# Spreading the block sums over the heads, and moving the meta rows' table and their part of the state, in a hybrid convolution and retention trunk

## The chip, the cores and the metric

The kernel runs on 1 core of one Trainium2 chip. The metric is the device time of one execution in microseconds (us); the time before is the median of 3 runs. In the profile PE is TensorE's matmuls, PEld its weight loads, DVE is VectorE, ACT ScalarE, POOL GpSimd and SP SyncE, which here only issues DMAs ("SPq" in a timeline).

## The reference

One decoder layer over 2048 rows of 1024 values, all f32. Sixteen learned "meta" rows are put in front of the sequence; they feed the branches and are not part of the output.

```python
hn = rms_norm(concat(meta, x), norm1_g)
cx, cb, cc, cg, q, k, v, rg = split(hn @ w_in, 8)        # w_in: 1024 x 4096
conv_out = cb * causal_conv3(cc * cx) * silu(cg)         # 512 channels
ret = head_group_norm(retention_chunkwise(rotary(q) * d**-0.5, rotary(k), v))
ret_out = ret * silu(rg)                                 # 4 heads of 128
y = h + concat(conv_out, ret_out) @ w_out
return rms_norm(y, final_g)[:, 16:]
```

Retention runs over chunks of 128 rows: inside a chunk with a decaying causal mask, between chunks through a 128 x 128 state for each head. The meta rows give every head's first state.

## The kernel before

**Products.** Activations lie transposed, 128 channels by 512 rows (HB). Each f32 operand is split into a high part and a low remainder (`split`, L85: an ACT copy that rounds, then a DVE subtraction, L114), and a product is three matmuls: low x high, high x low, high x high (L217 in `quad`, L273 in `quad_plain`). The split of a weight makes the tiles `wh` and `wl`, that of an activation `mh` and `ml`. `quad` computes a 2 x 2 block product with seven products in place of eight, as Strassen and Winograd do. For that it needs sums of blocks on both sides: those of the weights are made by POOL in `stationary` (four operations a quad, in place, in the buffers `ra` and `sa`), those of the activations by `block_sums`. A quad's results are taken out of PSUM by `take`; three of its banks are copied to tiles `tc` by ACT (L224), and PE may go on writing such a bank only after its copy.

**Order of work.** The 2048 rows are done in two halves, r = 0 and 1. In each half eight units follow one another, in the order of `UNITS`: units 0 to 3 are the retention heads (`head`), units 4 to 7 the groups of the convolution (`group_plain` for the first one, `conv_group` for the others). The first half begins with unit 4, and goes on with 0, 1, 2, 3, 5, 6, 7; the second runs from 0 to 7. A unit is two quads, plus, in a head, the small matmuls of retention, which mix with the next unit's first quad. After both halves the output projection follows (`output`, eight pairs of row blocks).

**Sums made ahead.** The activations' sums for the second half, and those of w_out for the output, are made while earlier units run. `prepare` (L183) is a generator with four steps. A step loads four blocks (L372 or L379), runs `block_sums` (with a scale, for x: one ACT multiplication, L178, three DVE operations of L175 and one subtraction; without, for w_out: four subtractions) and stores four results to DRAM (L191, `sums_x` or `sums_w`). The main loop draws steps from it at the end of a unit (L920 to L922): two at each unit from 3 up until the four are used up, and none at the unit with which the first half begins. In the first half these are the units 3 and 5, in the second 3 and 4. At the same place `conv_group` units of the first half draw the row factors of the second half: loads of x (L331) and squares on ACT (L332), four groups after unit 5. `prepared` (L194) loads the finished sums back (L201) and splits them.

**The meta rows in a head.** In the first half `ahead` loads the next unit's weights and multiplies the meta rows with them (`meta_products`, L408 on PE; the result is copied to the tile `mk`). `meta_state` (L423) loads the head's rotary table for the meta rows into a tile `mr` (L426; it shares the four buffers of the tag `tc`), adds up halves of the products (`meta_sums`, two L111), applies the rotary (L431 twice, L432, L111), multiplies keys and values on PE (L435) and copies the result to `state[h]` (L436). It is called behind the head's second quad (L681), but nothing holds its instructions there: the scheduler may put them on their engines' queues as soon as their operands are there.

**V across.** A head needs v with rows and channels exchanged. `part` (L599) splits the f32 values into planes of 16 bits (ACT, L602) and turns them with a transposing DMA (`cross`, L595, issued by SP); `join` puts them together again (L669). In the second half's first unit (`first` is given, L639) a `quad_plain` runs, `part` is called from its `take`, and after it `between` (L644) calls `prepared(m, sums_x, (0, 2))`, eight loads and splits for the second quad.

**Order.** Instructions are given in program order; a scheduler with a timing model sets the order of each engine's queue from priorities (program order), readiness and free buffers, and adds the semaphores. An engine runs its queue in order: what waits holds up all behind it. `tc.issue_after(i)` asks that the instructions of its block which run on i's engine are queued behind i; it waits for nothing itself. Buffers are shared by tag: `g` has 16 (`gen`), `ra` 8, `tc` 4.

The second quad's last gate product is L660, `sg[j] = pp * f[0]`, in the second `take` of `head`.

Of the kernel before, what the change touches and what calls it, by code (L numbers as in the profile page):

```python
# [8 lines left out]
F32 = mybir.dt.float32  # L9
# [4 lines left out]
ALU = mybir.AluOpType  # L14

P = 128
D = 1024
SEQ = 2048
NMETA = 16
KT = D // P  # L20
NG = 4
EPS = 1e-6
HB = 512
# [5 lines left out]
RING, RAW, GEN, COPIES = 3, 8, 16, 4  # L29
# [5 lines left out]
SUMS = (3, 2, 4, 6)  # L35

UNITS = (4, 0, 1, 2, 3, 5, 6, 7), (0, 1, 2, 3, 4, 5, 6, 7)


def retention_constants():  # L40
# [31 lines left out]
def hybrid_trunk(ctx: ExitStack, tc: tile.TileContext, t, out: bass.AP, chunk_decay):  # L72
# [5 lines left out]
    nc = tc.nc  # L78
# [4 lines left out]
    sb = ctx.enter_context(tc.tile_pool(name="sb", bufs=2))  # L83
# [100 lines left out]
    def prepare(load, dst, scale=None):  # L184

        for kt in range(KH):
# [4 lines left out]
                nc.sync.dma_start(dst[n, kt], a)  # L191
            yield

    def prepared(m, src, ns, held={}):  # L194

        for n in ns:
            for kt in range(KH):
                a = held.get((n, kt))
                if a is None:
                    a = gen("t")[:, :HB]  # L200
                    nc.sync.dma_start(a, src[n, kt])  # L201
                parts(m, SUMS[n], kt, a)

    copied = [None]
# [161 lines left out]
    def gain_of(k):  # L366
        return gain[:, k : k + 1]
# [52 lines left out]
        add(nc.vector, c, c, d)  # L420
        return a, c, b, d

    def meta_state(h, scratch):  # L423

        rot = sb.tile([P, HB], F32, name="mr", tag="tc", bufs=COPIES)[:NMETA, : 2 * P].rearrange("p (a c) -> p a c", a=2)
        nc.sync.dma_start(rot, t["rot_m"][h])  # L426
        k, v, a, b = meta_sums(scratch)
        half = P // 2
        lo, hi = slice(0, half), slice(half, P)
        for i, j in ((lo, hi), (hi, lo)):  # L430
            nc.vector.tensor_tensor(out=b[:, i], in0=k[:, j], in1=rot[:, 1, i], op=ALU.mult)  # L431
        nc.vector.tensor_tensor(out=a, in0=k, in1=rot[:, 0], op=ALU.mult)  # L432
        add(nc.vector, k, a, b)
        up = ps_misc()
        nc.tensor.matmul(up[:, :P], k, v, start=True, stop=True)  # L435
        nc.scalar.copy(out=state[h], in_=up[:, :P])  # L436
# [157 lines left out]
    def cross(across, apart):  # L594
        nc.sync.dma_start(  # L595
            across.bitcast(U16).rearrange("p (c f) -> p c f", c=2 * CH), apart.bitcast(U16), transpose=True
        )

    def part(a):  # L599

        apart, across = gen("pl")[:, :HB], gen("tr")[:, :HB]
        nc.scalar.copy(out=planes(apart), in_=halves(a))  # L602
        cross(across, apart)
        return across

    waiting = [[], []]
# [9 lines left out]
    def head(h, r, m, rot_t, f, turning, blocks, ahead, first=(), between=()):  # L616


        between = iter(between)
        k, v, late = [None, None], [None, None], []  # L620
        tables = [rot_t[:, :, j * HB : (j + 1) * HB] for j in range(2)]

        def take(i, j, pp, c):
            if i == 1 and c is None:
                v[j] = part(pp)
                return
            d = gen("kv")[:, :HB]
            if c is None:
                nc.scalar.copy(out=d, in_=pp)
            else:  # L630
                add(nc.vector, d, pp, c)
            if i == 0:
                rotary(d, tables[j])
                k[j] = d
            else:
                v[j] = d
                late.append(j)
# [3 lines left out]
        else:  # L641
            quad(stationary(blocks[0]), m, take)
            catch_up(0)
        next(between, lambda: None)()  # L644
        q, sg = [None, None], [None, None]

        def take(i, j, pp, c):
            d = gen("qg")[:, :HB]
            if i == 0:
                if c is None:  # L650
                    nc.scalar.copy(out=d, in_=pp)
                else:
                    add(nc.vector, d, pp, c)
                rotary(d, tables[j])
                q[j] = d
            else:
                if c is not None:
                    add(nc.vector, d, pp, c)
                    pp = d
                nc.vector.tensor_tensor(out=d, in0=pp, in1=f[0][:, j * HB : (j + 1) * HB], op=ALU.mult)  # L660
                sg[j] = d

        def split_late():
# [14 lines left out]
            join(1)  # L678
        next(between, lambda: None)()
        if blocks[1]:  # L680
            meta_state(h, blocks[1])  # L681
        blocks = ahead()
        states = [state[h]]
        vt = []
        for j in range(2):
# [12 lines left out]
            for c in range(CH - last):  # L698
                nxt = sb.tile([P, P], F32, name="state", tag="state", bufs=2 * CH)
                nc.vector.scalar_tensor_tensor(  # L700
                    out=nxt, in0=states[-1], scalar=chunk_decay[h], in1=up[:, c * P : (c + 1) * P],
# [4 lines left out]
        for j in range(2):  # L706
            sc = ps_misc()
            for c in range(CH):
# [4 lines left out]
                out=pm.rearrange("p (c i) -> p c i", c=CH), in0=sc.rearrange("p (c i) -> p c i", c=CH),  # L713
# [128 lines left out]
    for r in range(NR):  # L842
        f = factors[r]
        rot_t = sb.tile([P, 2, BLK], F32, name="rot_t", tag="rot_t", bufs=1)
        p0 = NMETA + r * BLK

        def load_tables():
            nc.sync.dma_start(rot_t, t["rot"][:, :, p0 : p0 + BLK])

        if r == 0:  # L850
            w = [None] * 4
            loads = w_loads(2 * NG)

            def begin(half):
                for n in (half, 2 + half):
                    w[n] = plain_part(n, loads[n], FIRST_W)

            m, b = moving(
                load_x(r), gain_of, {(0, 0): lambda: begin(0), (0, KH - 1): lambda: begin(1), (0, KT - 1): normalise_meta}
            )  # L860
            first = [[p for a, p in w]]
            blocks = None, meta_products([a for a, p in w])
            first.append(plain_parts(w_loads(2 * NG + 1)))
            load_tables()
            nc.sync.dma_start(cols, t["cols"])
            t3 = [a[:, i * HB : (i + 1) * HB] for a in (row_tile("t3", 1) for _ in range(2)) for i in range(2)]
            t1 = [brief("t1") if n < BRIEF else sb.tile([P, HB], F32, name="t1", tag="tc", bufs=COPIES) for n in range(KH)]
            for kt in range(KH):
                b11, b21, b12, b22 = (b[n * KH + kt] for n in range(4))
                block_sums(b11, b12, b22, b21, t1[kt], t3[kt], gain_of(kt), gain_of(KH + kt), nc.gpsimd)  # L870
                parts(m, 2, kt, b22)
                parts(m, 6, kt, b21)
            for _ in row_factors(0, f):
                pass
            nc.sync.dma_start(causal, t["causal"])
            nc.sync.dma_start(conv_w, t["conv_w"])
            nc.sync.dma_start(ret_g, t["ret_norm_g"])

            def late_parts():
                for i, held in ((3, t1), (4, t3)):  # L880
                    for kt in range(KH):
                        parts(m, i, kt, held[kt])

            between = ()
            later = prepare(load_x(1), sums_x, gain_of)
        else:
            m, b = moving(load_x(r), gain_of)
            first = [plain_parts(w_loads(0))]
            load_tables()
            prepared(m, sums_x, (1, 3))  # L890
            between = (lambda: prepared(m, sums_x, (0, 2)),)
            blocks = None, None
            later = prepare(load_w_out, sums_w)
        steps = row_factors(r + 1, factors[r + 1]) if r < NR - 1 else iter(())
        units = UNITS[r]
        turning = None
        special = (first, between)
        for n, unit in enumerate(units):
            following = units[n + 1] if n + 1 < len(units) else None
            rest = lambda: ahead(r, following, early=n == 0)  # L900
            if r + n == 0:
                blocks, completion = group_plain(unit - NG, m, f, blocks[1], first, late_parts, rest)
                special = (), completion
            elif unit < NG:
                if turning is None:
                    turning = [row_tile(name, 1 - r) for name in ("apart", "across")]
                blocks = head(unit, r, m, rot_t, f, turning, blocks, rest, *(special if unit == 0 else ()))
            else:
                if r == NR - 1 and following is None:
                    idle = sb.tile([P, 2, BLK], F32, name="held", tag="rot_t", bufs=1)  # L910
                    areas = [idle[:, 0], idle[:, 1], row_tile("held", 0), row_tile("held", 0)]
                    for i, a in enumerate(areas):
                        for j in range(2):
                            n, kt = 2 * (i // 2), i % 2 * 2 + j
                            held[n, kt] = a[:, j * HB : (j + 1) * HB]
                            nc.sync.dma_start(held[n, kt], sums_w[n, kt])
                blocks = conv_group(unit - NG, r, m, f, blocks, rest)
                for _ in range(4 - r):
                    next(steps, None)
            if NG - 1 <= unit and r + n > 0:  # L920
                next(later, None)
                next(later, None)  # L922

    m, b = moving(load_w_out)
# [42 lines left out]
```

## Time and profile before

| | |
|---|---|
| median of 3 runs | 887.63 us (886.71 to 888.54) |
| the profiled execution's own time | 887.77 us |
| its span, first to last instruction | 886.0 us |
| mean granted TensorE clock | 0.996 |
| DVE, ACT, POOL busy | 718.5, 472.3, 395.2 us |
| first half's heads, units 0 to 3 | from 57 to 245 us of the span |
| unit 5 of the first half | from 245 to 297 us |
| second half's units 0 to 3, unit 4 | from 378 to 561, from 561 to 608 us |

The page groups instructions by line, engine and operation; names such as `wl<-ra,wh` are tiles of the program, output first. A group's "idle" is time in which its engine did nothing just before its instructions, with what ended it. A timeline gives the start and duration of instructions in order, and in brackets the idle time before one and its releaser. Durations come from one profiled execution. Since PE is busy nearly throughout, idle time of the other engines costs nothing unless PE ends up waiting for it.

### The profile page before, as it was taken

The page shows a single profiled execution, that of the slowest core. Times are in us where ns is not written, and L with a number is a line of the kernel's source. Part 1 is how long each engine was busy: PE and PEld are TensorE (multiplying, and loading weights), DVE is VectorE, ACT ScalarE, POOL GpSimd, SP SyncE. Part 2 cuts the span into 40 slices and gives each one's busy share as a digit, 9 for nine tenths or more (in the row PEclk, how much of TensorE's full clock was granted, in tenths as well). Part 3 has the DMA queues.
Part 4 walks back from the last instruction along what each step waited for, and adds up shares of the span by engine and source line. Part 5 has one row for each costly group of instructions (what it writes and reads, how often), then busy time and mean ns, then how long its engine had stood idle before and what let it go on. Part 6 is the DMA issues. An engine that isn't in the chain of part 4 may idle for free.

```text
span 886.0 us, 12731 instructions
## 1 busy us (share of the span) xinstructions
PE 867.5 (98%) x4279; PEld 712.9 (80%) x4279; DVE 718.5 (81%) x1176; ACT 472.3 (53%) x871; POOL 395.2 (45%) x291
## 2 busy tenths in 40 slices
PE   8999999999999999999999999998999999999996
PEld 6778788878887778887888888887888888788885
DVE  6788888888897966998888898998767699766764
ACT  8665437373646463746464645534334476555553
POOL 0554241323145454451233323254547455877763
PEclk9999999999999999999999999999999999999999
DMA  9713223231577643935142423867221493555532
GB/s 338 235 56 80 72 62 91 66 96 48 141 264 224 205 153 79 293 124 158 48 103 65 91 77 78 268 194 256 60 72 53 136 381 108 177 157 180 165 112 91
DMA packets 110033, 125.31 MB, mean 141 GB/s; under 512 B 41424, under 2 KB 58128, under 8 KB 109968
## 3 DMA queue, kind: packets, MB, share of 16 engines
q1 hardware_dynamic: 109968, 124.50, 45.6%
q8 instruction: 34, 0.56, 0.3%
q14 instruction: 31, 0.25, 0.1%
HBM read 90.92 MB, written 25.17 MB: 131 GB/s over the span
## 4 chain that ended last, share of the span: by engine, by line
PE 74%; DVE 9%; DMA 3%; issue 3%; ACT 2%; POOL 1%; SPq 1%; POOLq 0%; DVEq 0%; ACTq 0%
PE pj L217 64%; PE pj L273 2%; PE ms L720 2%; DVE wl L114 2%; DVE ml L114 2%; PE ms L721 2%; PE ms L710 2%; PE ms L697 1%; DMA w<-in_w_out 1%; DVE x L175 1%; DVE c L470 1%; PE ms L408 1%; PE ms L688 1%; DVE w L114 1%; DMA n<-in_x 1%
## 5 line engine op out<-in xcount | busy, mean ns | idle before, releaser
L217 PE MATMUL pj<-mh,wl 128*128 128x512 f32 x1008 | 398.6, 396 | 6.6 <-ACT tc L224 2.8
L217 PE MATMUL pj<-ml,wh 128*128 128x512 f32 x1008 | 393.7, 391 | 1.1 <-DVE ml L114 1.1
L217 PE MATMUL pj<-mh,wh 128*128 128x512 f32 x1008 | 393.8, 391 | 0.0
L102 ACT CAST wh<-ra 128x512 fp32r<-128x512 f32 x216 | 133.7, 619 | 261.1 <-PE pj L217 217.2
L217 PEld LDWEIGHTS pj<-mh,wl 128*128 128x128 f32 x1008 | 189.7, 188 | 50.1 <-ACT tc L224 4.4
L217 PEld LDWEIGHTS pj<-mh,wh 128*128 128x128 f32 x1008 | 189.6, 188 | 40.1
L217 PEld LDWEIGHTS pj<-ml,wh 128*128 128x128 f32 x1008 | 189.7, 188 | 39.9 <-DVE ml L114 1.6
L114 DVE TENSOR_TENSOR wl<-ra,wh 128x512 fp32r<-128x512 f32 x216 | 185.2, 859 | 36.8 <-ACT wh L102 36.3
L114 POOL TENSOR_TENSOR ra<-ra 128x512 f32<-128x512 f32 x72 | 112.1, 1557 | 93.9 <-PE ms L408 42.4
L114 POOL TENSOR_TENSOR ra<-sa,ra 128x512 f32<-128x512 f32 x36 | 53.2, 1479 | 108.5 <-DVE wl L114 105.0
L111 POOL TENSOR_TENSOR sa<-ra 128x512 f32<-128x512 f32 x36 | 51.8, 1440 | 83.8 <-DMA ra<-in_w_in 32.4
L224 ACT COPY tc<-pj 128x512 f32<-128x512 f32 x108 | 62.6, 579 | 0.0
L273 PE MATMUL pj<-ml,mh 128*128 128x512 f32 x128 | 50.3, 393 | 0.0
L273 PE MATMUL pj<-mh,mh 128*128 128x512 f32 x128 | 50.1, 394 | 0.0
L273 PE MATMUL pj<-mh,ml 128*128 128x512 f32 x128 | 48.8, 398 | 0.1
L733 POOL TENSOR_TENSOR rp<-rs,neg_half 128x4 f32<-128x4 f32 x16 | 17.8, 1113 | 52.9 <-DVE rs L111 52.8
L783 DVE TENSOR_TENSOR yo<-pj,yo 128x512 f32<-128x512 f32 x32 | 21.9, 686 | 18.5 <-POOL yo L111 10.9
L533 POOL TENSOR_TENSOR c<-c,rr 128x512 f32<-128x512 f32 x14 | 27.6, 1973 | 20.7 <-DVE c L470 11.4
L785 ACT ACTIVATE rot<-yo 128x512 f32<-128x512 f32 x32 | 20.2, 630 | 30.7 <-DVE yo L783 30.3
L533 POOL TENSOR_TENSOR c<-c,tc 128x512 f32<-128x512 f32 x14 | 26.9, 1919 | 20.5 <-ACT tc L560 20.5
L102 ACT CAST wh<-sa 128x512 fp32r<-128x512 f32 x36 | 22.1, 615 | 23.4 <-PE pj L217 23.4
L788 POOL TENSOR_TENSOR z<-yo,final_g 128x512 f32<-128x512 f32 x16 | 26.9, 1684 | 16.5 <-DVE yo L783 16.5
(138 smaller groups left out, 1190.9 us busy)
## 6 DMA issues: line engine op xcount, KB each, us to landing
ra<-in_w_in SPq DMA_DIRECT2D x128, 256.0 KB, 2.8
x<-in_xT SPq DMA_DIRECT2D x48, 256.0 KB, 4.8
w<-in_w_out SPq DMA_DIRECT2D x32, 256.0 KB, 5.2
ra<-mixed SPq DMA_DIRECT2D x32, 256.0 KB, 2.9
yo<-in_x SPq DMA_DIRECT2D x32, 256.0 KB, 4.3
ra<-in_x SPq DMA_DIRECT2D x16, 256.0 KB, 3.3
mixed<-c SPq DMA_DIRECT2D x16, 256.0 KB, 2.6
mixed<-qg SPq DMA_DIRECT2D x16, 256.0 KB, 2.3
```

What stands on the lines that cost most here:

```text
L102: nc.scalar.copy(out=hi, in_=src)
L111: eng.tensor_tensor(out=out, in0=a, in1=b, op=ALU.add)
L114: eng.tensor_tensor(out=out, in0=a, in1=b, op=ALU.subtract)
L217: nc.tensor.matmul(bank, a[:, ks], b, start=first and kt == 0 and n == 0, stop=kt == KH - 1 and n == 2, skip_group_check=not first,)
L224: copied[0] = nc.scalar.copy(out=c, in_=bank)
L273: nc.tensor.matmul(banks[i], a[:, ks], b, start=half + kt + n == 0, stop=half == 1 and kt == KH - 1 and n == 2,)
L533: eng.tensor_tensor(out=out, in0=a, in1=b, op=ALU.mult)
L710: nc.tensor.matmul(sc[:, cs], k[j][:, cs], q[j][:, cs], start=True, stop=True)
L733: nc.gpsimd.tensor_tensor(out=rp, in0=rs, in1=neg_half.rearrange("p (c a) -> p c a", a=1), op=ALU.pow)
L783: last[0] = nc.vector.tensor_tensor(out=y, in0=pp, in1=y, op=ALU.add)
L785: nc.scalar.activation(junk, y, AF.Square, accum_out=ss[:, i, j : j + 1])
L788: nc.gpsimd.tensor_tensor(out=ys[i][j], in0=y, in1=final_g[:, j * HB : (j + 1) * HB], op=ALU.mult)
```

## The change

It has four parts. (1) `prepare` is drawn one step at a time, behind the units that `MAKES_SUMS` lists: in the first half units 0, 1, 2 and 5, in the second 0, 1, 2 and 4. (2) `mr` gets a tag and a tile of its own, and its load is issued at the top of `head`, ahead of the first quad. (3) `meta_state`'s instructions on DVE are queued behind the last gate product. (4) In the second half's first unit the two transposes of v are queued on SP behind the last of the eight loads of `prepared`.

```diff
+MAKES_SUMS = (0, 1, 2, 5), (0, 1, 2, 4)
...
+    loaded = [None]
+
     def prepared(m, src, ns, held={}):
...
-                    nc.sync.dma_start(a, src[n, kt])
+                    loaded[0] = nc.sync.dma_start(a, src[n, kt])
...
-    def meta_state(h, scratch):
-
-        rot = sb.tile([P, HB], F32, name="mr", tag="tc", bufs=COPIES)[:NMETA, : 2 * P].rearrange("p (a c) -> p a c", a=2)
+    def meta_table(h):
+        rot = sb.tile([P, 2, P], F32, name="mr", tag="mr", bufs=1)[:NMETA]
         nc.sync.dma_start(rot, t["rot_m"][h])
+        return rot
+
+    def meta_state(h, scratch, rot):
+
...
-    def part(a):
+    def part(a, to_cross=None):
...
-        cross(across, apart)
+        if to_cross is None:
+            cross(across, apart)
+        else:
+            to_cross.append((across, apart))
         return across
...
+        to_cross, gated = [], [None]
         k, v, late = [None, None], [None, None], []
+        rot = meta_table(h) if blocks[1] else None
...
-                v[j] = part(pp)
+                v[j] = part(pp, to_cross if len(first) else None)
...
         next(between, lambda: None)()
+        if to_cross:
+            with tc.issue_after(loaded[0].ins):
+                for pair in to_cross:
+                    cross(*pair)
...
-                nc.vector.tensor_tensor(out=d, in0=pp, in1=f[0][:, j * HB : (j + 1) * HB], op=ALU.mult)
+                gated[0] = nc.vector.tensor_tensor(out=d, in0=pp, in1=f[0][:, j * HB : (j + 1) * HB], op=ALU.mult)
...
         if blocks[1]:
-            meta_state(h, blocks[1])
+            with tc.issue_after(gated[0].ins):
+                meta_state(h, blocks[1], rot)
...
-            if NG - 1 <= unit and r + n > 0:
-                next(later, None)
+            if unit in MAKES_SUMS[r]:
                 next(later, None)
```

## The prediction

> **What bounds the kernel now.** I read the page's totals by engine first, then the waits of PE, then PE's timeline at every pause, then the other engines' timelines at the pauses that the change can touch.
>
> ```profile
> PE 867.5 (98%) x4279; PEld 712.9 (80%) x4279; DVE 718.5 (81%) x1176; ACT 472.3 (53%) x871; POOL 395.2 (45%) x291
> ```
>
> PE works for 867.5 us of a span of 886.0. The change removes no matmul, so all that it can win lies in the other 18.5 us. The waits of PE give 2.3 us at the start:
>
> ```profile
> PE ms L826 <- ACT warm L820: 2.3, 1, 2.3
> ```
>
> The timeline of PE shows the pauses inside. The bracket holds the idle time and what ended it.
>
> ```profile
> 63.31 0.50 PE L217 MATMUL pj<-mh,wl 128*128 128x512 f32 x1 [1.03 <-ACT tc L224]
> 94.46 0.46 PE L435 MATMUL ms<-mk 16*128 16x128 f32 x2 [0.94 <-DVE mk L111]
> 106.92 0.47 PE L217 MATMUL pj<-mh,wl 128*128 128x512 f32 x1 [0.54 <-DVE wl L114]
> 286.77 0.50 PE L217 MATMUL pj<-mh,wl 128*128 128x512 f32 x1 [1.81 <-ACT tc L224]
> 303.38 0.47 PE L217 MATMUL pj<-mh,wl 128*128 128x512 f32 x1 [0.72 <-ACT tc L560]
> 411.94 0.50 PE L217 MATMUL pj<-ml,wh 128*128 128x512 f32 x1 [1.14 <-DVE ml L114]
> 601.76 0.47 PE L217 MATMUL pj<-mh,wl 128*128 128x512 f32 x1 [1.85 <-DVE wl L114]
> 605.34 0.50 PE L217 MATMUL pj<-mh,wl 128*128 128x512 f32 x1 [0.60 <-DVE tc L111]
> ```
>
> These eight make 8.63 us. With the start that is 10.9 of the 18.5; the rest lies in shorter pauses and after the last product, where the change does nothing. PE is the bound, and the other engines count only where they make it pause: at the meta rows of unit 0 (94), at the turn from unit 0 to unit 1 (107), in unit 5 of the first half (287, 303), at the second quad of the second half's unit 0 (412), and in unit 4 of that half (602, 605). The most that the change can give is these seven, 7.6 us; the pause at 63 comes before all that it moves.
>
> **The change, part by part.**
>
> *The meta rows' table.* Four heads load it in the middle of their second quad, and DVE stands still for it:
>
> ```profile
> L431 DVE TENSOR_TENSOR mk<-mk,mr 16x64 f32<-16x64 f32 x8 | 1.4, 210 | 9.5 <-DMA mr<-in_rot_m 9.5
> 90.47 0.42 SPq L426 DMA_DIRECT2D mr<-in_rot_m  x1
> 92.85 0.35 DVE L431 TENSOR_TENSOR mk<-mk,mr 16x64 f32<-16x64 f32 x2 [2.18 <-DMA mr<-in_rot_m]
> ```
>
> The load goes out at 90.47 and is used at 92.85; four such waits make 9.5 us of DVE. Only in unit 0 does PE feel it, 0.94 us. With its own tile the load goes out at the head's top, more than a quad before its use; it is the same one DMA (0.42 us of SP) at a place where SP is not pressed. Taken: -0.94, and nothing in units 1 to 3, whose DVE wait PE did not feel.
>
> *The meta rows' part moves* behind the last gate product (L660), the end of the second quad: six small DVE operations, then L435 on PE and a copy on ACT. Nothing needs the state at once; the first update of it comes after a product of retention. But the place is a different one. Here is the turn from unit 1 to unit 2, DVE and then POOL:
>
> ```profile
> 147.56 0.68 DVE L660 TENSOR_TENSOR qg<-pj,rr 128x512 f32<-128x512 f32 x1
> 148.16 1.75 DVE L586 TENSOR_TENSOR qg<-qg,rot 128x512 f32<-128x512 f32 x1
> 149.83 1.58 DVE L111 TENSOR_TENSOR mk<-mk 16x128 f32<-16x128 f32 x2
> ...
> 148.07 1.29 POOL L114 TENSOR_TENSOR ra<-ra 128x512 f32<-128x512 f32 x1 [15.42 <-PE ms L408]
> 149.44 1.62 POOL L114 TENSOR_TENSOR ra<-sa,ra 128x512 f32<-128x512 f32 x1
> 151.14 1.43 POOL L114 TENSOR_TENSOR ra<-ra 128x512 f32<-128x512 f32 x1
> ```
>
> L586, which adds two operands in SBUF, takes 1.75 us here, and ends 0.55 after POOL's first operation does; a pair of tiny adds takes 1.58 us. The same kind of work in the middle of the quad:
>
> ```profile
> 140.58 0.27 DVE L432 TENSOR_TENSOR mk<-mk,mr 16x128 f32<-16x128 f32 x1
> 140.89 0.28 DVE L111 TENSOR_TENSOR mk<-mk 16x128 f32<-16x128 f32 x1
> ...
> 143.35 0.48 PE L435 MATMUL ms<-mk 16*128 16x128 f32 x2
> ```
>
> Free of POOL the six operations cost 0.48 (the pair of sums at 104.50, below), 2 x 0.21, 0.27 and 0.28, together 1.45 us. Behind POOL's three the first starts at about 149.8, the pair ends at 151.4, the third waits until 152.6, and the last ends near 153.4. After L660 (148.24) and a free L586 (0.68) it would have been 150.4: the move puts up to 3.0 us more between gate and L435. L435 stands in PE's queue, and all matmuls of the next unit's first quad queue behind it; whether PE pauses depends on where the scheduler puts it. Today it stands 2.2 us behind its operand (141.17 to 143.35). Bounds: nothing, and 4 x 3.0. I take 0.15 for each of four heads, +0.6, the side of the row of today, as its 2.2 covers most of the 3.0.
>
> [...]
>
> In the turn from unit 0 to 1 DVE is the late one already:
>
> ```profile
> 99.38 0.68 DVE L660 TENSOR_TENSOR qg<-pj,rr 128x512 f32<-128x512 f32 x1
> 101.10 3.48 DVE L483 TENSOR_TENSOR c<-c,cb 128x512 f32<-128x512 f32 x2
> 104.50 0.48 DVE L111 TENSOR_TENSOR mk<-mk 16x128 f32<-16x128 f32 x2
> 104.90 1.28 DVE L483 TENSOR_TENSOR c<-c,cb 128x512 f32<-128x512 f32 x2
> ```
>
> Unit 4's four closing products lie between the gate and the split for which PE waits 0.54 us at 106.9. The change puts 1.45 us ahead of that split and takes 0.48 away (the next head's two sums), +0.97. Against it stands that DVE no longer loses 2.18 us at 92.85, of which 0.94 only moves PE along: it reaches this turn about 0.8 us less late, since after that it has to wait for PE again. Taken: +0.3; bounds -0.54 (the pause gone) and +3.5 (a whole step of the sums, below, ahead of the split too).
>
> *The sums.* A step for the second half's x is three operations of L175, one L114 and one ACT multiplication; a step for the output weights is four of L114:
>
> ```profile
> L175 DVE SCALAR_TENSOR_TENSOR x<-x,gain 128x512 f32<-128x512 f32 x16 | 13.6, 858 | 0.7 <-ACT x L178 0.6
> L114 DVE TENSOR_TENSOR x<-x 128x512 f32<-128x512 f32 x4 | 3.8, 946 | 0.0
> L178 ACT ACTIVATE x<-x,gain 128x512 f32<-128x512 f32 x8 | 5.7, 716 | 0.0
> L114 DVE TENSOR_TENSOR w<-w 128x512 f32<-128x512 f32 x16 | 13.1, 845 | 0.0
> ```
>
> That is 3 x 0.858 + 0.946 = 3.5 us of DVE and 0.7 of ACT for x, and 4 x 0.845 = 3.4 of DVE for w; each with four loads and four stores of 256 KB on SP, which move with it. Now two steps stand behind unit 3 and two behind unit 5 (first half) or 4 (second). Then there is one behind each of units 0, 1, 2 and one behind 5 or 4. The heads have room on the whole, 7.5 us of DVE in unit 1's stretch:
>
> ```profile
> 148.28:196.46 48.18, 48.18 (x277) 40.35 (x276) 40.66 (x82) 26.16 (x46) 13.83 (x12) 1.00 0.31 77
> ```
>
> (columns: PE, PEld, DVE, ACT, POOL busy). A step of 3.5 us fits in twice; unit 5's own first quad today takes two such steps with only a short pause. I charge +0.4 for all six heads, bounds 0 and 2.0 (a pause of 0.3 in each).
>
> What unit 5 gets back: at 287 PE waited for an ACT copy (L224) with squares, a SiLU and one multiplication of the sums ahead of it.
>
> ```profile
> L332 ACT ACTIVATE n<-n 128x512 f32<-128x512 f32 x16 | 10.0, 627 | 4.3 <-DMA n<-in_x 4.3
> 285.02 0.71 ACT L178 ACTIVATE x<-x,gain 128x512 f32<-128x512 f32 x1
> 286.14 0.58 ACT L224 COPY tc<-pj 128x512 f32<-128x512 f32 x1
> ```
>
> Half of the 16 squares stay in this unit, and so does one step; but DVE comes to it 7 us less loaded from unit 3, and one of two steps goes. The pause at 303 hangs on DVE, which loses 3.5 us of work in the 20 us before. Of 1.81 + 0.72 = 2.53 us I take -1.4; bounds 0 and -2.53.
>
> In unit 4 the sums lie directly in front of the split for which PE waits at 601.8:
>
> ```profile
> 594.62 1.19 DVE L114 TENSOR_TENSOR w<-w 128x512 f32<-128x512 f32 x1
> 598.03 2.98 DVE L114 TENSOR_TENSOR w<-w 128x512 f32<-128x512 f32 x3
> ```
>
> These four operations take 4.17 us; half of the eight in this unit go, about 2.1 us. Of 1.85 + 0.60 = 2.45 I take -1.6; bounds 0 and -2.45.
>
> *The transposes of the second half's unit 0.* SP now stands before the second transpose until ACT has split the planes, with the eight loads of the sums behind it:
>
> ```profile
> 400.65 1.01 ACT L602 COPY pl<-pj 128x1024 uint16<-128x1024 uint16 x1
> ...
> 401.69 1.24 SPq L595 DMA_TRANSPOSE tr<-pl  x1
> 402.98 3.90 SPq L201 DMA_DIRECT2D t<-sums_x  x8
> ...
> 411.45 1.36 ACT L669 COPY v<-tr 128x1024 uint16<-128x1024 uint16 x1
> ```
>
> With both transposes behind the loads, these go out at least 1.24 us earlier, more than the 1.14 that PE waits at 411.9. The transposes end at the latest at 401.7 + 3.9 + 2 x 1.24 = 408.1, 3.3 us ahead of their first reader at 411.45, so nothing takes the pause's place. Taken: -0.9 of 1.14, as the casts and splits between are in queues with other work; bounds 0 and -1.14.
>
> The sum: -0.94 + 0.6 + 0.3 + 0.4 - 1.4 - 1.6 - 0.9 = -3.5 us. The profiled execution took 887.77, 0.14 more than the median 887.63; it would become 884.2, the median 884.1.
>
> **The rivals.**
>
> *L435 stops PE at each turn (slower).* The six operations end behind POOL, and the matmul stands in PE's queue ahead of that. Price 4 x 3.0 = 12.0 in place of my 0.6: 895.5. From 1.0 us for each head the change gives nothing, from 1.5 it is slower by what can be told. For it: the 1.75 and 1.58 us rows. Against it: the 2.2 us that L435 has behind its operand today, and PE does not wait at this turn for the splits, which suffer likewise. Chance 0.12.
>
> *The pauses only move (no change).* Unit 5 keeps its eight squares and one step, unit 4 its closing chain; what they lose comes back in the heads. Then the sums give 0 instead of -3.0: 887.1. For it: DVE is 81% busy everywhere. A form of it is that the change does not do what it says: the loads of sums wait for buffers, the transposes stand behind them, and 0.9 more is lost. Chance 0.22.
>
> *Every pause after 63 us goes.* 7.6 us: 880.0. For it: DVE gains 9.5 us of waiting besides. Against it: it needs all seven, that at 107 included. Chance 0.10.
>
> **How the numbers follow.** The forecast has 0.56. A measurement of this kernel can tell about 0.2%, 1.8 us: faster is below 885.9, slower above 889.4. Faster takes the last rival's 0.10 and 0.52 of the forecast's, 0.62; the same takes 0.22 and most of the rest, 0.25; slower 0.13. The range leaves out most of the first rival and half of the last: 880.9 to 889.0.
>
> **What would show it.** Right: no DVE wait for mr; the pauses at 94, 412, 602 and 605 gone, that at 287 under 1.2 us, none new over 0.5 us in units 0 to 3. Wrong: L435 with a PE wait for DVE mk at several turns; a PE wait for a split in units 0 to 2 longer than 0.54 us; or the pause at 287 as long as before, which would say that the squares made it, not the sums.

## The result, and the profile after

The changed kernel takes 902.39 us (median of 4 runs, 901.77 to 904.29), the one before in the same comparison 887.88. The ratio is 1.0162, 95% interval 1.0149 to 1.0175: slower by 14.5 us, where 3.5 us less were forecast. It lies above the top of the range (889.0) and above the first rival's price (895.5). The profiled execution took 901.77 us.

The page of the kernel after, its totals:

```profile
PE 869.6 (97%) x4279; PEld 714.6 (79%) x4279; DVE 706.2 (78%) x1176; ACT 472.7 (53%) x871; POOL 392.7 (44%) x291
```

The span is 900.0 us, 14.0 more. PE is idle for 30.4 us in place of 18.5, +11.9; and it is busy for 2.1 us more with the same 4279 matmuls (see the clock, last section). DVE is busy for 12 us less, so it is not DVE's work that grew. The waits of PE name the idle time (total, times, longest):

```profile
PE pj L221 <- DVE wl L116: 8.4, 6, 2.2
PE ms L714 <- ACT kd L707: 7.3, 4, 1.8
```

(L113, L116, L221, L228, L412, L442, L705 and L714 after are L111, L114, L217, L224, L408, L435, L688 and L697 before; kd is made by ACT from the transposes of k, L707.) The wait for kd is new, and comes four times: once behind each head of the first half. Four of the six waits for wl are the same four turns. PE's timeline at the turn from unit 1 to unit 2 of the kernel after:

```profile
157.12 0.39 PE L221 MATMUL pj<-mh,wh 128*128 128x512 f32 x1
157.44 0.48 PE L442 MATMUL ms<-mk 16*128 16x128 f32 x2
157.85 1.07 PE L412 MATMUL ms<-ra,meta_s 128*16 128x128 f32 x32
158.85 0.66 PE L705 MATMUL ms<-ident,kv 128*128 128x128 f32 x4
161.33 1.16 PE L714 MATMUL ms<-v,kd 128*128 128x128 f32 x8 [1.82 <-ACT kd L707]
162.32 0.60 PE L705 MATMUL ms<-ident,kv 128*128 128x128 f32 x4
164.87 0.50 PE L221 MATMUL pj<-mh,wl 128*128 128x512 f32 x1 [1.95 <-DVE wl L116]
```

And the same turn of the kernel before, L408, L688 and what follows:

```profile
143.76 0.63 PE L408 MATMUL ms<-ra,meta_s 128*16 128x128 f32 x16
147.31 0.63 PE L408 MATMUL ms<-ra,meta_s 128*16 128x128 f32 x16
147.87 0.66 PE L688 MATMUL ms<-ident,kv 128*128 128x128 f32 x4
148.28 0.48 PE L217 MATMUL pj<-mh,wl 128*128 128x512 f32 x1
...
153.85 1.05 PE L697 MATMUL ms<-v,kd 128*128 128x128 f32 x8
```

Before, the next unit's meta products and the transposes of k ran inside the second quad and at its end (143.8 to 148.3), *ahead* of the next unit's first two products. These, 24 matmuls and 5.5 us, then covered what follows from the small ones: POOL may change the weight blocks once the meta products have read them, and makes the third product's weights; ACT makes kd from the transposes. After, both stand *behind* the two products, and both behind L442. The cover is spent when they begin, and PE waits for kd, and then for the split weight.

POOL, ACT and DVE of the kernel after at this turn, one timeline each:

```profile
159.06 1.26 POOL L116 TENSOR_TENSOR ra<-ra 128x512 f32<-128x512 f32 x1 [20.47 <-PE ms L412]
...
157.96 0.27 ACT L443 COPY state<-ms 128x128 f32<-128x128 f32 x1 [3.15 <-PE ms L442]
160.58 0.69 ACT L707 ACTIVATE kd<-ms,cols 128x512 f32<-128x512 f32 x1
...
155.29 0.27 DVE L113 TENSOR_TENSOR mk<-mk 16x128 f32<-16x128 f32 x1
```

POOL stands idle for 20.5 us until the meta products are done. The six DVE operations were through at 155.6, 1.9 us before L442 begins: they are not what anyone waits for.

### The profile page after: what moved, and what is told of

It reads as the page before. It is cut to its first block, busy times and chain, and to the rows that moved or that the text cites. A ratio compares the mean times of both kernels' runs of the same rounds, so it can differ in the third digit from the quotient of the medians.

```text
span 900.0 us, 12715 instructions
## 1 busy us (share of the span) xinstructions
PE 869.6 (97%) x4279; PEld 714.6 (79%) x4279; DVE 706.2 (78%) x1176; ACT 472.7 (53%) x871; POOL 392.7 (44%) x291
## 4 chain that ended last, share of the span: by engine, by line
PE 85%; DVE 7%; ACT 3%; issue 2%; DMA 1%; POOL 1%; SPq 1%; POOLq 0%; DVEq 0%; ACTq 0%
PE pj L221 70%; PE pj L277 7%; DVE ml L116 2%; PE ms L727 2%; PE ms L738 1%; PE ms L737 1%; DVE wl L116 1%; PE ms L714 1%; PE ms L412 1%; DMA x<-in_xT 1%; DVE rot L591 1%; DMA n<-in_x 1%; POOL yo L113 0%; PE ms L307 0%; ACT mk L418 0%
## 5 line engine op out<-in xcount | busy, mean ns | idle before, releaser
L221 PE MATMUL pj<-mh,wl 128*128 128x512 f32 x1008 | 399.4, 396 | 11.4 <-DVE wl L116 8.4
L221 PE MATMUL pj<-ml,wh 128*128 128x512 f32 x1008 | 394.2, 391 | 0.0
L221 PE MATMUL pj<-mh,wh 128*128 128x512 f32 x1008 | 394.1, 391 | 0.0
L116 DVE TENSOR_TENSOR wl<-ra,wh 128x512 fp32r<-128x512 f32 x216 | 186.2, 863 | 62.1 <-ACT wh L104 61.6
L221 PEld LDWEIGHTS pj<-mh,wl 128*128 128x128 f32 x1008 | 190.1, 189 | 55.4 <-DVE wl L116 9.2
L221 PEld LDWEIGHTS pj<-mh,wh 128*128 128x128 f32 x1008 | 190.1, 189 | 40.2
L221 PEld LDWEIGHTS pj<-ml,wh 128*128 128x128 f32 x1008 | 190.2, 189 | 38.5 <-issue 0.5
L116 POOL TENSOR_TENSOR ra<-ra 128x512 f32<-128x512 f32 x72 | 112.0, 1556 | 112.8 <-PE ms L412 78.0
L116 POOL TENSOR_TENSOR ra<-sa,ra 128x512 f32<-128x512 f32 x36 | 51.8, 1440 | 98.3 <-DVE wl L116 98.0
L113 POOL TENSOR_TENSOR sa<-ra 128x512 f32<-128x512 f32 x36 | 52.7, 1463 | 89.2 <-DVE wl L116 40.2
L228 ACT COPY tc<-pj 128x512 f32<-128x512 f32 x108 | 62.5, 579 | 0.1
```

What stands on the lines that cost most here:

```text
L113: eng.tensor_tensor(out=out, in0=a, in1=b, op=ALU.add)
L116: eng.tensor_tensor(out=out, in0=a, in1=b, op=ALU.subtract)
L221: nc.tensor.matmul(bank, a[:, ks], b, start=first and kt == 0 and n == 0, stop=kt == KH - 1 and n == 2, skip_group_check=not first,)
L228: copied[0] = nc.scalar.copy(out=c, in_=bank)
```

## The experiments

**Theory A** (formed from these rows): the small matmuls share the four PSUM banks of the tag `ms`, and the scheduler hands out a tag's buffers in program order. L442 writes such a bank and stands in the program ahead of the next unit's meta products and of the transposes of k. Behind the gate it cannot take its bank early, so they cannot take theirs. **Theory B** is the first rival: DVE's six operations are late because POOL holds them up. **Theory C**: the spread sums overload the turns.

**The gate undone.**

```diff
-            with tc.issue_after(gated[0].ins):
-                meta_state(h, blocks[1], rot)
+            meta_state(h, blocks[1], rot)
```

> The changed kernel with one part undone: the state's part of the meta rows is no longer queued behind the last gate product; the table's own tile, the spread sums and the transposes behind the loads stay. Theory A (banks in program order): the state's product L442 takes one of the four banks of the tag ms, the banks are handed out in program order, so the next unit's meta products (L412) and the transposes of k (L705) cannot go ahead of it, and the gate drags them all behind the next unit's first two products. Without the gate the four pairs of pauses (kd 1.8 and wl 1.6 to 2.2 us) go: 14.5 us less than the changed kernel or a little more, 884 to 888 us. Theory B (POOL holds up the six small DVE operations at the turn): the same, 884 to 890. Theory C (the spread sums overload the turns): the pauses for wl stay, 896 to 902.

Measured: 885.62 us, ratio to before 0.9974 (0.9962 to 0.9985). The eight pauses at the turns are gone. Two of 1.2 us, for pm, stand in heads, where the kernel before had none above 0.2; pm is the masked product of retention, which DVE makes. The gate is worth 16.7 us here, the quotient of the two ratios, 1.0189, and theory C falls: the sums stayed spread.

**The gate alone**, on the kernel before (`gated` is set at L660):

```diff
         if blocks[1]:
-            meta_state(h, blocks[1])
+            with tc.issue_after(gated[0].ins):
+                meta_state(h, blocks[1])
```

> The kernel before with one part added: the gate. The table is still loaded in the middle, in the shared tag, and the sums stand at their old places. Theory A: all of the loss is there, 899 to 904 us, with a pause for kd of about 1.8 us and one for wl of about 2 at each of the four turns. Theory B: the same or less, as POOL works at these turns in any case, 896 to 904. Theory C: no loss, 886 to 890.

Measured: 909.12 us, 1.0234 (1.0206 to 1.0262): all of the loss, and more than any theory had. The waits of PE in this run:

```profile
PE pj L217 <- DVE wl L114: 9.9, 5, 2.7
PE ms L699 <- ACT kd L692: 7.3, 4, 1.8
```

These are the same pairs. The excess over the changed kernel has two visible parts: the pauses that the other parts of the change take away remain (at 312, 430 and 620), and PE is busy for 873.7 us, 4.1 more than after (four slow stretches of the clock against two, see the last section).

**The meta products first in the program.**

```diff
-        if blocks[1]:
+        current, blocks = blocks, ahead()
+        if current[1]:
             with tc.issue_after(gated[0].ins):
-                meta_state(h, blocks[1], rot)
-        blocks = ahead()
+                meta_state(h, current[1], rot)
```

> The changed kernel with the gate kept, but the next unit's weight loads and meta products stand ahead of the state's part in program order, so that they get their bank first. Theory A: the meta products go back into the second quad, POOL starts at once, the pauses for wl (1.6 to 2.2 us, four of them) go; the transposes of k still come behind L442 and a pause for kd may stay: 885 to 894 us. Theory B: the six DVE operations stand where they stood, behind POOL, which starts earlier and so holds them up more: no gain, 898 to 906. Theory C: 898 to 904.

Measured: 888.83 us, 1.0012 (1.0002 to 1.0022). Two statements are exchanged, the gate stays, and 13.3 us are back (1.0012 over 1.0162 is 0.985). The waits of PE:

```profile
PE pj L221 <- DVE wl L116: 5.0, 4, 2.6
PE ms L442 <- DVE mk L113: 1.4, 1, 1.4
```

No wait for kd is left, though I had thought that one may stay. The transposes do stand behind L442 still, but both now come ahead of the next unit's two products (L705 at 155.29 at the turn from unit 1 to 2), which cover kd until 161.05. Of the four waits for wl one is at a turn (252, 1.4 us) and one in unit 5 (303, 2.6 us). Theory B, which had no gain here, falls. A wait of L442 for mk, 1.4 us, is there once, but it is little of theory B's mechanism: POOL is through at 151.27, and of the 3.9 us from the gate (150.83) to the last of the six operations (154.76), 2.7 are four other instructions of DVE that stand between them.

**A bank of its own**, gate kept, program order as in the change:

```diff
-        return ps.tile([P, HB], F32, name="ms", tag="ms", bufs=4)
+        return ps.tile([P, HB], F32, name="ms", tag="ms", bufs=3)
...
-        up = ps_misc()
+        up = ps.tile([P, HB], F32, name="us", tag="us", bufs=1)
```

> The changed kernel with the gate kept, and a PSUM bank of its own for the state's product; the other small matmuls share three banks in place of four. Theory A: nothing stands behind L442 for want of a bank, both kinds of pause go, 883 to 889 us; three banks may cost up to 3 us in retention. Theory B: DVE's six operations are late as before, so the loss stays: 896 to 903. Theory C: 896 to 903.

Measured: 883.20 us, 0.9949 (0.9933 to 0.9964), with the next run the fastest of the study. PE's timeline about the turn from unit 1 to 2 in this run:

```profile
147.83 1.05 PE L714 MATMUL ms<-v,kd 128*128 128x128 f32 x8
148.72 0.60 PE L705 MATMUL ms<-ident,kv 128*128 128x128 f32 x4
...
155.63 0.48 PE L442 MATMUL us<-mk 16*128 16x128 f32 x2
```

L442 comes as late behind the gate as in the kernel after (155.63, 5.2 us from the start of the gate product at 150.48; 4.8 there), and nothing waits behind it: unit 1's second four transposes of k and its first state products stand 7 us ahead of it. A late L442 costs nothing that can be seen here when it holds no shared bank; what the gate itself costs is the next comparison.

**The bank without the gate**: the last kernel with the call of the first experiment.

> The changed kernel with a bank of its own for the state's product, and without the gate. Against the run with the bank and the gate this gives the gate's own worth once the bank does not tie the small matmuls to it. Theory A says that the gate then costs nothing by itself; the prediction had +0.6 for it from POOL's hold on the six operations: equal within 2 us, 882 to 886. If POOL's hold did matter, this one is faster than the one with the gate by 1 us or more.

Measured: 883.62 us, 0.9946 (0.9933 to 0.9958): equal to the run with the gate. The gate, for which the sum had +0.6 because of POOL's hold on the six operations, is worth nothing that can be told. In the run with bank and gate there is no such hold at this turn: POOL's third operation ends at 149.90, before the gate.

**Gate and bank on the kernel before, and the bank alone** (the edits above, without the other parts):

> The kernel before with the gate, and with a PSUM bank of its own for the state's product (three for the other small matmuls). With the run that has the gate alone this makes a square of gate and bank without the other parts. Theory A: the gate's 21 us are gone, 886 to 890. If something else in the gate cost time (DVE behind POOL at the turns, the late state), a good part stays: 895 or more.

> The kernel before with nothing but the bank of its own for the state's product. The square's fourth corner. Theory A: without the gate no small matmul waited for a bank much, so the bank alone is worth little: 885.5 to 888.5. If it is 884 or less, what the versions with the bank gain comes from the bank and not from the change's parts.

Measured: 887.88 us, 0.9994 (0.9985 to 1.0002), and 890.50 us, 1.0022 (1.0014 to 1.0031; outside what I expected, on the slow side; that three banks for the rest are a little too few may be the reason, which no run shows apart). The square, as ratios to the kernel before:

| | bank shared | own bank |
|---|---|---|
| no gate | 1 | 1.0022 |
| gate | 1.0234 | 0.9994 |

The gate costs 2.3% with the bank shared and nothing with its own; there the kernel with the gate is even 0.3% faster than the one without, for a reason that stays open (with the change's other parts the two are equal, 0.9949 and 0.9946). That is theory A, without the sums, the table or the transposes.

**The state later in the program**: behind the meta products, the first four transposes of k and kd; gate kept, bank shared.

```diff
             nc.scalar.mul(kd, tp, kd_col[:, h : h + 1])
+            if j == 0 and current[1]:
+                with tc.issue_after(gated[0].ins):
+                    meta_state(h, current[1], rot)
```

> The changed kernel with the gate kept and the bank shared, but the state's part stands later in program order: behind the next unit's meta products and behind the first four transposes of k and the copy kd, just ahead of the first update that needs it. Theory A: neither the meta products nor the first transposes stand behind L442; the pauses for kd and wl go; the second transposes still do, and may cost a little: 883 to 889 us.

Measured: 888.19 us, 0.9999 (0.9990 to 1.0007), at the upper end. The pauses for kd and wl at the turns are gone, as theory A has it. In their place stands something close to the first rival, and small. A wait of PE in this run:

```profile
PE ms L442 <- DVE mk L113: 2.5, 3, 1.0
```

And its timelines of DVE and then POOL before the turn from unit 1 to 2:

```profile
146.95 1.66 DVE L590 TENSOR_TENSOR rot<-qg,rot_t 64x512 f32<-64x512 f32 x1
148.63 1.69 DVE L591 TENSOR_TENSOR rot<-qg,rot_t 64x512 f32<-64x512 f32 x1
...
146.44 1.62 POOL L116 TENSOR_TENSOR ra<-sa,ra 128x512 f32<-128x512 f32 x1
148.14 1.62 POOL L116 TENSOR_TENSOR ra<-ra 128x512 f32<-128x512 f32 x1
```

POOL works at the turn again, two rotary operations of DVE take 1.66 and 1.69 us beside it (0.69 for L591 at 151.89 in the kernel after, where POOL is idle), the gate comes late, and L442 waits for mk at three turns, 2.5 us together. So POOL delays DVE ahead of the gate here, and not the six operations behind it: it is through at 149.76, and the gate starts at 151.62. Two more pauses of over 1 us are left, 1.91 in unit 5 and 1.41 for pm.

**The other parts, each alone on the kernel before** (the diff's lines of that part only).

> The kernel before with one part added: the sums drawn at units 0, 1, 2 and 5, and 0, 1, 2 and 4. The prediction's terms: -1.4 in unit 5, -1.6 in unit 4, +0.4 in the heads and part of +0.3 at the turn from unit 0 to 1: -2.3 us, the pauses at 287 and 602 shorter and no new ones; 884.5 to 887. Rival (the pauses only move into the heads): within 1 us of before.

Measured: 0.9994 (0.9985 to 1.0003), no gain. PE's pauses of this run that answer to the prediction's terms:

```profile
118.88 0.49 PE L722 MATMUL ms<-v,pm 128*128 128x128 f32 x2 [0.98 <-DVE pm L714]
216.47 0.49 PE L722 MATMUL ms<-v,pm 128*128 128x128 f32 x2 [0.88 <-DVE pm L714]
289.52 0.50 PE L219 MATMUL pj<-mh,wl 128*128 128x512 f32 x1 [1.81 <-ACT tc L226]
```

Two new pauses stand in heads, in retention (pm, which DVE makes), and that at the turn from unit 0 to 1 grew from 0.54 to 1.20. That in unit 4 shrank from 1.85 to 0.39. The rival is right here: the pauses move. In unit 5 the pause for the ACT copy is as long as before, 1.81. The two copies of ACT about it in this run, and then the same two in the run with gate and own bank and the sums at their old places (the last one below), where PE has no such pause:

```profile
280.38 0.58 ACT L226 COPY tc<-pj 128x512 f32<-128x512 f32 x1
...
288.89 0.57 ACT L226 COPY tc<-pj 128x512 f32<-128x512 f32 x1
```

```profile
278.46 0.58 ACT L228 COPY tc<-pj 128x512 f32<-128x512 f32 x1
...
283.59 0.58 ACT L228 COPY tc<-pj 128x512 f32<-128x512 f32 x1
```

In the first, seven squares (L334), a copy of planes and one multiplication of the sums stand between the two, as in the kernel before; in the second four squares do, and the rest comes behind. So the pause goes with what the scheduler has put ahead of the copy in ACT's queue, mostly squares, and not with where the sums are drawn, which are spread in the first run and at their old places in the second. No run moved the squares alone.

> The kernel before with one part added: in the second half's first unit the two transposes are queued behind the loads of the sums. The prediction's term: -0.9 us, the pause of 1.14 us at 412 goes. Rival: the casts and splits are late for another reason and the pause stays; 0.

Measured: 0.9980 (0.9971 to 0.9989), -1.8 us. The pause at 412 is gone. It is more than the 1.14 of that pause, though the interval reaches down to -1.0; in the profiled executions the clock differs too (last section). Why it is more stays open.

> The kernel before with one part added: the table's tile and its early load, without the gate. The prediction's term: -0.94 us, the pause of PE at 94 goes with the DVE waits for mr. Rival: with the table early the six small operations are queued early in unit 0, and the pause at the turn to unit 1 grows by what is won; 0.

Measured: 1.0004 (0.9995 to 1.0013), nothing. The pauses at 63, 94 and 107 are gone from the trace and PE is idle for 16.4 us of the span of 887.4, 2.1 less than before; but it is busy for 871.0 us, 3.5 more. The clock doesn't explain that, as each of the two executions has one slow stretch (last section); it stays open.

**The spread sums where the turns are free**: gate and own bank, sums at their old places.

> The changed kernel with the bank of its own and the gate, but the sums drawn at their old places, two steps at units 3 and 5, and 3 and 4. Against the run with the bank and the gate this gives the worth of the spread sums where the turns are not blocked. The sums alone gave nothing on the kernel before (pauses moved into the heads): if that holds here, 882.5 to 884. If the spread pays once the turns are free, 885 to 887, with the pauses at 287 and 602 back.

Measured: 885.70 us, 0.9969 (0.9959 to 0.9979), against 0.9949 with the spread: the spread pays about 2 us here, though the two intervals touch (0.9959 to 0.9964). A wait of PE of this run that the spread takes away, in unit 4 (one of the two is 1.89 us, at 598):

```profile
PE pj L221 <- DVE wl L116: 2.7, 2, 1.9
```

The pause at 287, which I had expected back as well, did not come.

## Why the prediction was wrong, point by point

- **What bounds the kernel.** Right: PE, and only its pauses count. The idle time explains 11.9 of the 14.0 us; the other 2.1 are busy time, with two slow stretches of the clock (from 112 and from 217) in place of one (from 288).
- **The step that failed: "the meta rows' part moves".** It followed the part's own six operations, its matmul and the need for the state, and priced only how late these come: +0.6 us. It asked who queues behind L435 on PE, and not who waits for the bank that L435 fills. The next unit's meta products and the transposes of k do, by the order in which banks are handed out, and POOL and ACT wait for these. The runs show 16.7 us on the changed kernel and 2.3% on the one before, and none with a bank of its own.
- **The first rival** had the place (the four turns) and the sign, but not the mechanism. The six operations were free of POOL, because POOL itself stood still until the meta products; from the gate (152.60) to 155.56 they took 3.0 us, with two rotary operations between them. L442 waited for mk once, 0.76 us, in unit 0. Of the prediction's signs of being wrong the one that came was the wait for a split: 2.18, 1.95 and 1.77 us behind units 0 to 2.
- **DVE beside POOL**, which spoke against the change (the rows of 1.75 and 1.58 us), was seen again: a rotary operation of DVE that meets POOL takes 1.66 and 1.69 us above, against 0.69 where POOL is idle. It did not decide the result: the same change moved POOL away, and where POOL was back, L442 waited 2.5 us in all.
- **The table**, -0.94: the pause went, the time did not. The DVE stall of 9.5 us was worth nothing that can be told.
- **The transposes**, -0.9: right in mechanism, measured -1.8 (-1.0 to -2.6).
- **The sums**, -1.4 - 1.6 + 0.4: on the kernel before 0. The term for unit 4 fits (its two pauses went from 2.45 to 0.91 us), though on the way to it half of eight operations was put at 2.1 us, where the four shown take 4.17. That for unit 5 failed at the pause of 1.81 us, which stayed with the order of ACT's queue, and the heads and the turn from unit 0 to 1 paid 2.5 us of new pauses in place of 0.4. So the second rival was right about the sums, as long as they are alone; its price of 887.1 should have been 886.7, as the three terms make -2.6 and not -3.0. Where the turns are free the spread pays about 2 us.
- **The sum without the gate.** With the 0.6 out it was -4.1; measured -2.3 without the gate, and -4.5 with gate and bank. That the last comes near is partly luck: the table alone gave 0 for -0.94, and the transposes alone -1.8 for -0.9. The third rival's -7.6 was reached by no run.

## What to carry to other kernels

Where buffers are handed out in program order, as here, to hold back an operation holds back the buffer that its result goes to, and with it what comes later in the program and takes its buffer from the same few. Before queueing a step later, list the tags of its outputs, and who is next in them; give it a buffer of its own or move it in the program behind those who must not wait. And look at what the late step's neighbours feed: here two small matmuls kept POOL and ACT from starting under cover of 5.5 us of products.

## What the runs showed of the hardware

Some pauses of PE were followed by a lower granted clock in these executions, and so cost more than their length. Here are windows of the kernel after around the turn from unit 2 to 3 (columns: PE, PEld, DVE, ACT, POOL busy with counts, then the granted clock, the DMA share and GB/s):

```profile
204.00:211.00 7.00, 7.00 (x60) 5.46 (x59) 6.36 (x14) 1.64 (x5) 0.00 (x0) 1.00 0.64 226
215.00:222.00 7.00, 5.22 (x14) 4.01 (x14) 4.94 (x10) 1.00 (x2) 2.41 (x3) 0.53 0.33 75
```

After two pauses of 1.82 and 1.77 us within 5.4 us the granted clock is 0.53, and the next matmuls start every 0.43 us in place of 0.23; some eleven of them lose about 2.2 us. It does not follow each pause: the turn from unit 1 to 2 has the same pair (1.82 and 1.95 us) and keeps 1.00. The same pause, 1.85 us in unit 4 of the kernel before and 1.88 with the table alone, is followed by

```profile
602.00:608.00 6.00, 5.40 (x24) 4.09 (x24) 6.00 (x11) 1.29 (x3) 1.31 (x1) 1.00 0.90 307
```

in the first and, in the second, by

```profile
602.00:608.00 6.00, 6.00 (x19) 4.79 (x20) 6.00 (x11) 1.53 (x3) 1.08 (x1) 0.72 0.85 277
```

so the second execution does some nine matmuls slowly, about 1.6 us, and the first none. At 287 it is the kernel before that is slow (pause of 1.81 us, clock 0.68 from 286.7 to 292), while the run with the transposes alone is not (1.53 us, clock 1.00):

```profile
286.70:292.00 5.30, 5.29 (x23) 4.38 (x24) 5.30 (x9) 5.25 (x10) 0.90 (x1) 1.00 0.96 264
```

So the same pause has two outcomes, and what decides between them no run shows. It is not the length alone: a slow stretch followed single pauses of 1.81 and 1.88 us, and none followed that of 1.85. A difference of 2 us between two profiled executions of this kernel may be the clock's alone, as one slow stretch lost about 2.2 us and another about 1.6, and single parts are to be judged by their repeated runs. Counted by runs of matmuls 0.43 us apart, the profiled execution of the kernel before has one such stretch (from 288), the kernel after two (from 112 and 217), the gate alone four (from 110, 216, 271 and 623), the table alone one (from 603) and the transposes alone none. With the gate alone it adds up: its four executions took 905.54 us at a mean clock of 0.994, 908.13 at 0.991, and 910.11 and 910.53 at 0.987. So part of the gate's 2.3% goes with the clock, but the fastest of them is still 17.5 us above the kernel before (888.01).
